# Two-layer encoder trunk on one core: direct part of the output product by pairs of row blocks, and three preparations of the second layer formed later

## The chip, the core and the metric

The kernel runs on one core of one Trainium2 chip. TensorE (PE in the profile) multiplies matrices and transposes, PEld loads its weights, VectorE (DVE) and ScalarE (ACT) work on elements, GpSimd (POOL) does small arithmetic and the DMAs that add, SyncE (SP) issues most other DMAs. The metric is the device time of one execution in microseconds (us): the median of the runs of a kernel.

## The reference

512 tokens of width 1024 go through two layers in float32. Each layer norms the tokens, projects them once into mixer heads, memory queries and gates, attends (layer one: three dilated windows; layer two: grouped queries with 2-D rotary tables), attends to 256 memory tokens, gates the heads and adds an output product to the residual stream:

```python
for i in range(DEPTH):
    h = rmsnorm(x, norm_g[i])
    mem_h = rmsnorm(mem, mem_norm_g[i])
    ...
    o_mem = memory_attention(q_mem, mem_h, w_mem_kv[i], mem_qn_g[i], mem_kn_g[i])
    y = jnp.concatenate([o_mix, o_mem], axis=-1) * jax.nn.silu(gate)
    x = x + jnp.einsum('bse,ed->bsd', y, w_out[i])
```

`y` is 512 x 1536 and `w_out[i]` is 1536 x 1024.

## The kernel before

**Numbers.** Every float32 operand of a product is split into a high part (ACT rounds it to fp32r) and a low part (DVE subtracts the high part from the original). A product is then three matmuls: high by high, low by high, high by low. For weights this is the cast `wh<-wl` (L295) and the split `wo<-wl,wh` (L305), once for each piece of 128 x 1024; a ring of four such pairs is live (`RING`).

**Strassen.** Products of 1024 columns in the inner dimension are done by quarters with seven products instead of eight (`s_chunk`): 12, 11, S1, S2, S4, S3, 22, in this order on PE. The token side needs sums of quarters (`first_t`, `diffs_t`, `rest_t`: S1 = 21 - 22, S2 = S1 - 11, S4 = S2 + 12, S3 = 11 - 21), the weight side needs T1 to T4, formed in part by DMAs that add (POOL, L260 to L279). S4 is the fifth product. Between products ACT copies a PSUM bank out (L372) and DVE adds others (L389); S2 adds into the bank that held 11, so it waits until L389 has read that.

**The output product.** The 1536 columns of `y` are taken as 1024 by Strassen and as 512 directly (`out_rest`). Strassen's results are added by DMAs into `acc`, four row blocks b of 128 tokens in two column halves n (L876). The direct part is eight groups of twelve matmuls, one for each (n, b), and DVE adds each to `acc[b][n]` (L756). Its weights are two pieces for each n, called O1 in `PLAN`; the loop runs over n and inside it over b, through `chunk`. When both halves of a block are there, `ev_o` stores the block (x1d, SP), norms it (`norm_1`: squares on ACT L475, root on POOL L477, L436, L437; `norm_2`: DVE L482), has PE transpose it (xT, L488) and builds the token side of layer two: blocks 0 and 1 give the quarters 11 and 12 (`first_t`: casts and low parts named h, copies named f), blocks 2 and 3 the differences.

**Start of layer two.** While this goes on, PE projects the memory to K and V (`mem_kv`, weights T2b: four pieces each for K and V, and for each of them two groups for either of two row blocks). K's blocks are normed (`head_sq`, `head_mul`: xn L578), transposed (qT) and split (`put_norm`, low part L634); V's are split at once (L656, L657). Then the first Strassen set of layer two follows, the memory queries. `setup_b` multiplies the rotary tables by the gains of q and k (L1279, L1282); their first reader is the rotation in the second set (L1336).

**What sets the order.** The program is written by a driver in slots: each group or product ends in `drv.tick()`, which runs the generators that are due; `yield n` puts a generator off by n slots. Each engine executes its instructions in the order so written. `Weights` plans loads, sums, casts and splits by the number g of the slot in which each piece is used last and needed first.

Of the kernel before, what the change touches and what calls it, by code (L numbers as in the profile page):

```python
# [13 lines left out]
ALU = mybir.AluOpType  # L14
# [6 lines left out]
QS = 128 ** -0.5  # L21
TCKW = {}
NBIG, NM4, NS2, SCRATCH = 7, 23, 14, 2048
RING, LEAD = 4, 2
BULK, ACTIVE, SET_AT, WARM, MEM_B, PREP_Y, ACC_AT, PREP_B, HALF, SET_B = 2, 2, 15, 1, 12, 1, 4, 1, {"a": 3, "b": 3, "o": 0}, 1
MEM_STEP = 1, 1
MEM_D = 4
PD = 2
EO = 2, 2, 1, 2, 2, 1
YB = {"m": (2, 2), "k": (1, 1, 1), 0: (1, 2, 1), 1: (1, 2, 1)}  # L30
# [95 lines left out]
def trunk_kernel(ctx: ExitStack, tc: tile.TileContext, x, mem, wall, norm_g, mem_norm_g, gcol,  # L126
                 qn_a, kn_a, qn_b, kn_b, ident_d, mask_d, tab_a, tab_b, out):
    nc = tc.nc
# [7 lines left out]
    drv = Driver()  # L136
# [31 lines left out]
    def mm_early(o, a, b, c, d, start):  # L168

        T.matmul(o, a, b, start=start, stop=False, skip_group_check=True)  # L170
        T.matmul(o, c, d, start=False, stop=False, skip_group_check=True)  # L171

    def mm_late(o, a, b, stop):
        T.matmul(o, a, b, start=False, stop=stop, skip_group_check=True)  # L174
# [15 lines left out]
    class Weights:  # L190
        def __init__(self):
            self.items, self.last, self.need, self.allocs, self.sums = [], [], [], [], []
            self.users = {}
            g = 0
            for c in SEQ:
                kind, d = PLAN[c], sum(pieces(k) for k in PLAN[:c])
                base = len(self.items)
                if kind in GROUPS:
                    units, nb = GROUPS[kind]
                    for u in range(units):  # L200
                        for x in (2 * u, 2 * u + 1):
                            self.items.append((c, "P", x))
                            self.last.append(g + (u + 1) * nb - 1)
                            self.allocs.append(((c, "P", x), d, kind))
                            self.users[c, "P", x] = 1
                            d += 1
                        self.need += [base + 2 * u + 2] * nb
                    g += units * nb
                else:
                    n = 1 if kind in ("W1", "W1b", "W1bs") else 2  # L210
                    at = {k: d + i * n for i, k in enumerate(("21", "11", "12", "22"))}
                    self.allocs += [((c, k, x), at[q] + x, kind) for k, q in LOADS for x in range(n)]
# [128 lines left out]
    def chunk(units, nb, group, evac, pre=None):  # L341

        ps = [None] * nb
        for u in range(units):
            w = []
            for h, l in (W.take(), W.take()):
                w += [(h[:, k * 512:(k + 1) * 512], l[:, k * 512:(k + 1) * 512]) for k in range(2)]
            for b in range(nb):
                if u == 0:
                    ps[b] = pj()  # L350
                if pre:
                    pre(u, b)
# [194 lines left out]
        V.tensor_tensor(s3, full["11", c], p, ALU.subtract)  # L547
        split(*slot(H, "S1", c), s1)

    def rest_t(H, c, ds):  # L550

        def put(k, f):
            hi, lo = slot(H, k, c)
            A.copy(hi, f)
            drv.late(lambda: V.tensor_tensor(lo, f, hi.bitcast(F32), ALU.subtract))

        s1, s2_, s4, s3, f22 = [full.pop((k, c)) for k in ("S1", "11", "12", "S3", "22")]
        V.tensor_tensor(s2_, s1, s2_, ALU.subtract)
        V.tensor_tensor(s4, s4, s2_, ALU.add)
        put("S2", s2_)  # L560
        yield ds[0]
        put("S4", s4)
        yield ds[1]
        put("S3", s3)
        yield ds[2]
        put("22", f22)
        yield 1
# [60 lines left out]
            yield 1  # L628
        Ms[layer] = M

    def put_norm(q, gain, hi, lo):

        drv.late(lambda: A.activation(hi, q, AF.Copy, scale=gain))
        drv.soon(lambda: V.scalar_tensor_tensor(lo, q, gain, hi.bitcast(F32), ALU.mult, ALU.subtract))  # L634
        yield 1

    def mem_kv(layer, M, pre=None):
        kt_ = [m4(F32R, "kmT").rearrange("p (h t) -> p h t", h=4) for _ in range(2)]
        vt_ = [m4(F32R, "vm").rearrange("p (b e) -> p b e", b=2) for _ in range(2)]

        def ev_k(b, p):
            r = head_sq(p)

            def rest():
                xn = head_mul(p, r)
                yield 2
                q = transpose4(xn)
                cs = slice(b * 128, (b + 1) * 128)
                yield from put_norm(q, gk_m[layer], kt_[0][:, :, cs], kt_[1][:, :, cs])

            drv.release(rest(), 2)
            yield 1

        def ev_v(b, p):

            A.activation(vt_[0][:, b], p, AF.Copy, scale=0.5)  # L656
            V.scalar_tensor_tensor(vt_[1][:, b], p, 0.5, vt_[0][:, b].bitcast(F32), ALU.mult, ALU.subtract)  # L657
            yield 1

        proj_t(M, NAT[:2], ev_k, pre)  # L660
        proj_t(M, NAT[:2], ev_v)
        return kt_, vt_
# [79 lines left out]

    def out_rest(ys, acc, done, evac):

        for n in range(2):
            def group(w, u, b, p):
                cs = slice(b * 128, (b + 1) * 128)
                while any(y is None for y in ys):
                    drv.tick()
                for k in range(4):  # L750
                    mm_early(p, ys[k][0][:, cs], w[k][0], ys[k][0][:, cs], w[k][1], k == 0)
                for k in range(4):
                    mm_late(p, ys[k][1][:, cs], w[k][0], k == 3)

            def ev(b, p, n=n):
                V.tensor_tensor(acc[b][n], p, acc[b][n], ALU.add)  # L756
                yield 1
                while (n, b) not in done:
                    yield 1
                yield from evac(n, b, acc[b])  # L760
            chunk(1, 4, group, ev)


    def gates(od, o_done):

# [485 lines left out]
    def ev_o(n, b, x1):  # L1251
        if n:
            for j in range(2):
                nc.sync.dma_start(x1d[b][:, j * 512:(j + 1) * 512], x1[j])
            r = norm_1(x1)
            yield EO[0]
            norm_2(x1, r, rows["x1"])
            yield EO[1]
            if b < 2:
                first_t(H2, x1, b)  # L1260
            else:
                yield from diffs_t(H2, x1, b - 2)
                yield EO[2]
                yield from rest_t(H2, b - 2, EO[3:])

    drv.spawn(mem_norm(1), MEM_B)
    out_proj(YW, ys, xv, ev_o, lambda: [m4(name="acc") for _ in range(2)])
# [1 line left out]


    ropeB = pool.tile([128, 2048], F32, tag="tabs", name="tabs", bufs=1).rearrange("p (a c b e) -> p a c b e", a=2, c=2, b=4)
    tb_raw = s2(name="tbraw").rearrange("p (c b e) -> p c b e", c=2, b=4)
    nc.sync.dma_start(tb_raw, tab_b.rearrange("p (c b e) -> p c b e", c=2, b=4))
    grB = s2(name="grB")[:, 0:256].rearrange("p (a e) -> p a e", a=2)
    nc.sync.dma_start(grB[:, 0], qn_b.to_broadcast([128, 128]))
    nc.sync.dma_start(grB[:, 1], kn_b.to_broadcast([128, 128]))

    def setup_b():
        V.tensor_scalar(grB[:, 0], grB[:, 0], QS, None, ALU.mult)  # L1279
        for qk in range(2):  # L1280
            for cs_ in range(2):
                V.tensor_tensor(ropeB[:, qk, cs_].rearrange("p b (h e) -> p b h e", h=2),  # L1282
                                tb_raw[:, cs_, :, None, :].to_broadcast([128, 4, 2, 64]),
                                grB[:, qk].rearrange("p (h e) -> p h e", h=2)[:, None].to_broadcast([128, 4, 2, 64]), ALU.mult)
                yield 1
# [289 lines left out]
```

## Time and profile before

| | |
|---|---|
| median of three runs | 966.98 us (965.21 to 967.11) |
| profiled execution | 968.3 us, of which the span is 966.5 us |
| granted TensorE clock, mean | 0.996 |
| PE busy | 946.8 us, 98% of the span |
| DVE, ACT, POOL busy | 82%, 71%, 35% of the span |
| direct part, layer one | about 619 to 644 us from the span's start |
| memory K and V of layer two | 644 to 672 us |
| first Strassen set of layer two | 672 to 699 us |

Times in the profile count from the start of the span. A row of the timeline gives start, duration, engine, line, operation, out<-in and shape; a bracket at its end gives the idle time of the engine before it and what ended it. Lines are those of the kernel before; in the changed kernel the same code stands 1 to 33 lines further down.

### The profile page before, as it was taken

To read this page: it belongs to the slowest core of one execution; us is meant where nothing else is said; L and a number is where in the kernel's file an instruction comes from. 1 tells how busy PE (TensorE), PEld (TensorE's weight loads), DVE (VectorE), ACT (ScalarE), POOL (GpSimd) and SP (SyncE) were. 2 spreads that over 40 slices of the span, in tenths; PEclk is the share of its full clock that TensorE was granted. 3 is DMA by queue.
4 is the path that set the end of the run, shared out by engine and by line. 5 is a ranking of instruction groups with operands and counts; after the bars stand their busy time and mean duration, and the time that the engine had idled before them with its cause. 6 is when DMAs were issued, how large, how long until landed. Compare 5 with 4: busy or idle time off the path is not lost.

```text
span 966.5 us, 16604 instructions
## 1 busy us (share of the span) xinstructions
PE 946.8 (98%) x5682; PEld 833.2 (86%) x5682; DVE 791.4 (82%) x1411; ACT 681.7 (71%) x1701; POOL 341.4 (35%) x482
## 2 busy tenths in 40 slices
PE   8999999999999999999999999999899999999998
PEld 5879888888888888888899997788899999998886
DVE  5898676878888888888888999769878898769883
ACT  5775689686868686868685657546768977879770
POOL 1512423557554545454726011322332330111010
PEclk9999999999999999999999999999899999999999
DMA  9989956969686868685959889889766687777744
GB/s 360 317 235 327 271 116 172 294 120 268 149 258 143 262 150 258 154 261 132 283 132 241 266 206 297 268 242 366 167 157 129 199 235 179 207 204 190 206 131 131
DMA packets 89129, 209.81 MB, mean 217 GB/s; under 512 B 25298, under 2 KB 36050, under 8 KB 89044
## 3 DMA queue, kind: packets, MB, share of 16 engines
q1 hardware_dynamic: 69892, 145.76, 43.4%
q0 software_dynamic: 17856, 60.83, 33.4%
q10 hardware_dynamic: 1296, 2.16, 0.6%
q8 instruction: 45, 0.74, 0.3%
q14 instruction: 40, 0.33, 0.1%
HBM read 157.27 MB, written 12.65 MB: 176 GB/s over the span
## 4 chain that ended last, share of the span: by engine, by line
PE 80%; DVE 8%; DMA 6%; ACT 3%; issue 2%; POOL 1%; SPq 0%; DVEq 0%; POOLq 0%; ACTq 0%
PE pj L170 21%; PE pj L171 21%; PE pj L174 20%; DVE wo L305 2%; PE qT L585 2%; PE sa L1106 1%; PE oo L1208 1%; PE pt L1187 1%; PE sa L1102 1%; PE ptb L1405 1%; DMA og<-odb 1%; DMA acc<-sn 1%; DMA wl<-wl 1%; DMA grB<-in_qn_b_dram 1%; DMA od<-o 1%
## 5 line engine op out<-in xcount | busy, mean ns | idle before, releaser
L305 DVE TENSOR_TENSOR wo<-wl,wh 128x1024 fp32r<-128x1024 f32 x255 | 315.1, 1242 | 6.0 <-ACT wh L295 5.8
L295 ACT CAST wh<-wl 128x1024 fp32r<-128x1024 f32 x255 | 268.5, 1060 | 29.3 <-PE pj L171 18.9
L170 PE MATMUL pj<-wh,hS 128*128 128x512 f32 (+1 forms) x448 | 159.0, 368 | 3.9 <-DVE sn L389 3.9
L171 PE MATMUL pj<-wh,hS 128*128 128x512 f32 (+1 forms) x448 | 153.6, 356 | 0.0
L170 PE MATMUL pj<-wh,h 128*128 128x512 f32 (+1 forms) x336 | 117.9, 365 | 0.0
L171 PE MATMUL pj<-wh,h 128*128 128x512 f32 (+1 forms) x336 | 114.0, 353 | 0.0
L437 POOL TENSOR_TENSOR rstd<-mse,half 128x4 f32<-128x4 f32 (+2 forms) x98 | 103.1, 1052 | 8.2
L174 PE MATMUL pj<-wo,hS 128*128 128x512 f32 (+1 forms) x448 | 100.8, 355 | 2.0 <-DVE wo L305 2.0
L170 PEld LDWEIGHTS pj<-wh,hS 128*128 128x128 f32 x448 | 85.9, 192 | 14.8 <-issue 2.6
L171 PEld LDWEIGHTS pj<-wh,hS 128*128 128x128 f32 x448 | 86.1, 192 | 10.3
L372 ACT COPY sn<-pj 128x512 f32<-128x512 f32 x132 | 73.1, 590 | 29.7 <-PE pj L174 29.7
L436 POOL TENSOR_SCALAR mse<-hss 128x4 f32<-128x4 f32 (+1 forms) x86 | 45.1, 525 | 132.2 <-ACT junk L573 128.0
L174 PEld LDWEIGHTS pj<-wo,hS 128*128 128x128 f32 x448 | 75.3, 191 | 14.5 <-DVE wo L305 2.7
L573 ACT ACTIVATE junk<-sn 128x128 f32<-128x128 f32 x264 | 79.1, 308 | 4.1 <-DVE sn L383 4.1
L1050 POOL TENSOR_TENSOR ta<-sn,tabs 128x128 f32<-128x128 f32 (+1 forms) x64 | 37.4, 592 | 118.6 <-DVE sn L578 92.0
L389 DVE TENSOR_TENSOR sn<-pj,sn 128x512 f32<-128x512 f32 x99 | 67.7, 686 | 12.3 <-PE pj L174 11.8
L174 PE MATMUL pj<-wo,h 128*128 128x512 f32 (+1 forms) x336 | 74.8, 352 | 0.0
L171 PEld LDWEIGHTS pj<-wh,h 128*128 128x128 f32 x336 | 63.8, 190 | 7.4
L170 PEld LDWEIGHTS pj<-wh,h 128*128 128x128 f32 x336 | 63.6, 189 | 7.4 <-DVE sn L389 0.2
L279 POOL DMA_DIRECT2D wl<-wl x33 | 29.1, 881 | 111.9 <-DVE wo L305 56.0
L174 PEld LDWEIGHTS pj<-wo,h 128*128 128x128 f32 x336 | 56.0, 189 | 8.7
L578 DVE TENSOR_TENSOR sn<-sn,rstd 128x512 f32<-128x512 f32 (+1 forms) x82 | 48.0, 594 | 7.2 <-POOL rstd L437 7.2
(235 smaller groups left out, 2335.1 us busy)
## 6 DMA issues: line engine op xcount, KB each, us to landing
wl<-in_wall_dram SPq DMA_DIRECT2D x222, 512.0 KB, 7.0
wl<-wl POOLq DMA_DIRECT2D x66, 512.0 KB, 5.5
wl<-in_wall_dram POOLq DMA_DIRECT2D x42, 512.0 KB, 8.5
acc<-sn POOLq DMA_DIRECT2D x16, 256.0 KB, 4.8
od<-o SPq DMA_DIRECT2D x12, 256.0 KB, 5.6
og<-od SPq DMA_DIRECT2D x12, 256.0 KB, 5.5
odb<-o SPq DMA_DIRECT2D x12, 256.0 KB, 3.4
og<-odb SPq DMA_DIRECT2D x12, 256.0 KB, 4.2
```

The lines of the kernel that those rows point to most:

```text
L170: T.matmul(o, a, b, start=start, stop=False, skip_group_check=True)
L171: T.matmul(o, c, d, start=False, stop=False, skip_group_check=True)
L174: T.matmul(o, a, b, start=False, stop=stop, skip_group_check=True)
L295: A.copy(wh, self.tile[self.items[i]])
L305: V.tensor_tensor(wo, self.tile[key], wh.bitcast(F32), ALU.subtract)
L372: A.copy(t, b)
L389: V.tensor_tensor(t, b, t, ALU.subtract if q == "12" else ALU.add)
L436: G.tensor_scalar(e, ss, EPS, None, ALU.add)
L437: G.tensor_tensor(r, e, half[:, 0:n], ALU.pow)
L573: A.activation(jk, p[:, j * 128:(j + 1) * 128], AF.Square, scale=QS, accum_out=ss[:, j:j + 1])
L578: V.tensor_tensor(xn[:, 0:n], p.rearrange("p (a b) -> p a b", a=4)[:, 0:n], r[:, 0:n, None].to_broadcast([128, n, 128]), ALU.mult)
L1050: G.tensor_tensor(ta[:, 0:n], xn[:, 0:n, 0:32], ropeA[:, 0, b, s0:s0 + n], ALU.mult)
```

## The change

1. `out_rest` runs over pairs of row blocks first, then over n, then over the two blocks. All four O1 pieces are taken in its first four groups and stay in use until the sixth and eighth group; the planner counts so.
2. `rest_t` of layer two adds S4 one slot later, in a slot of its own.
3. The low part of memory K in layer two comes five slots later, that of V's second block three.
4. The tables: their DMAs are issued inside `setup_b`, which starts at slot 9 instead of 1 after the output product, and the multiplications come four slots after that, k's before q's.

```diff
-BULK, ..., SET_B = ..., 1
+BULK, ..., SET_B = ..., 9
+LO_K, LO_V = (0, 5), (0, 3)
...
                     units, nb = GROUPS[kind]
+                    if kind == "O1":
+                        n = PLAN[c - 1] == "O1"
+                        for x in range(2):
+                            self.items.append((c, "P", x))
+                            self.last.append(g + 5)
...
+                        self.need += [base + 2] * 2 if not n else [base + 2] * 6
+                        g += 2 if not n else 6
+                        units = 0
...
-    def rest_t(H, c, ds):
+    def rest_t(H, c, ds, spread=False):
...
-        V.tensor_tensor(s4, s4, s2_, ALU.add)
+        if not spread:
+            V.tensor_tensor(s4, s4, s2_, ALU.add)
         put("S2", s2_)
-        yield ds[0]
+        if spread:
+            yield ds[0] - 1
+            V.tensor_tensor(s4, s4, s2_, ALU.add)
+            yield 1
...
-    def put_norm(q, gain, hi, lo):
+    def put_norm(q, gain, hi, lo, wait=0):
         drv.late(lambda: A.activation(hi, q, AF.Copy, scale=gain))
+        if wait:
+            yield wait
         drv.soon(lambda: V.scalar_tensor_tensor(lo, q, gain, hi.bitcast(F32), ALU.mult, ALU.subtract))
...
             A.activation(vt_[0][:, b], p, AF.Copy, scale=0.5)
+            if b and LO_V[layer]:
+                yield LO_V[layer]
...
     def out_rest(ys, acc, done, evac):
-        for n in range(2):
...
-            chunk(1, 4, group, ev)
+        ws = []
+        for bs in ((0, 1), (2, 3)):
+            for n in range(2):
+                if len(ws) == n:
+                    ws.append([])
+                    for h, l in (W.take(), W.take()):
+                        ws[n] += [(h[:, k * 512:(k + 1) * 512], l[:, k * 512:(k + 1) * 512]) for k in range(2)]
+                w = ws[n]
+                for b in bs:
...
+                    drv.release(ev(n, b, p), 2)
+                    W.advance()
+                    drv.tick()
...
-    tb_raw = s2(name="tbraw").rearrange("p (c b e) -> p c b e", c=2, b=4)
-    nc.sync.dma_start(tb_raw, tab_b.rearrange("p (c b e) -> p c b e", c=2, b=4))
...
     def setup_b():
-        V.tensor_scalar(grB[:, 0], grB[:, 0], QS, None, ALU.mult)
-        for qk in range(2):
+        tb_raw = s2(name="tbraw").rearrange("p (c b e) -> p c b e", c=2, b=4)
+        nc.sync.dma_start(tb_raw, tab_b.rearrange("p (c b e) -> p c b e", c=2, b=4))
...
+        yield 4
+        for qk in (1, 0):
+            if not qk:
+                V.tensor_scalar(grB[:, 0], grB[:, 0], QS, None, ALU.mult)
```

The order on three places, before and after. On DVE from the direct part to the norms of the blocks (acc<-pj the sums, acc<-acc,rstd the norms, wo the weight splits, tabs and grB the tables), before:

```order
L756 TENSOR_TENSOR acc<-pj,acc 128x512 x4
L305 TENSOR_TENSOR wo<-wl,wh 128x1024 x2
L482 TENSOR_SCALAR acc<-acc,rstd,row 128x512 x2
L1279 TENSOR_SCALAR grB<-grB 128x128
L1282 TENSOR_TENSOR tabs<-tbraw,grB 128x512
L482 TENSOR_SCALAR acc<-acc,rstd,row 128x512 x2
L1282 TENSOR_TENSOR tabs<-tbraw,grB 128x512
L305 TENSOR_TENSOR wo<-wl,wh 128x1024 x2
```

and after, from the same place:

```order
L767 TENSOR_TENSOR acc<-pj,acc 128x512 x4
L316 TENSOR_TENSOR wo<-wl,wh 128x1024 x2
L493 TENSOR_SCALAR acc<-acc,rstd,row 128x512 x2
L767 TENSOR_TENSOR acc<-pj,acc 128x512
L493 TENSOR_SCALAR acc<-acc,rstd,row 128x512 x2
L767 TENSOR_TENSOR acc<-pj,acc 128x512
L316 TENSOR_TENSOR wo<-wl,wh 128x1024 x2
L162 TENSOR_TENSOR h_7826<-xT,h_7826 128x4x128
```

The tables are gone from here, and the norms of blocks 0 and 1 stand among the last two sums of the direct part.

On ACT in the same place (sq the squares of a block, wh the weight casts, h and f the casts and copies of `first_t`, junk the squares of memory K), before:

```order
L475 ACTIVATE sq,ss<-acc 128x512 x4
L295 COPY wh<-wl 128x1024 x2
L475 ACTIVATE sq,ss<-acc 128x512 x2
L158 COPY h_7898<-xT 128x4x128
L158 COPY h_7906<-xT 128x4x128
L537 COPY f_7914<-xT 128x512
L537 COPY f_7916<-xT 128x512
L573 ACTIVATE junk,hss<-pj 128x128 x4
```

and after (h_7826 comes twice, for block 0 and for block 1):

```order
L306 COPY wh<-wl 128x1024 x2
L159 COPY h_7826<-xT 128x4x128
L159 COPY h_7834<-xT 128x4x128
L548 COPY f_7842<-xT 128x512
L548 COPY f_7844<-xT 128x512
L486 ACTIVATE sq,ss<-acc 128x512 x2
L306 COPY wh<-wl 128x1024 x2
L159 COPY h_7826<-xT 128x4x128
```

Block 0's casts and copies now stand ahead of the squares of blocks 2 and 3; before they stood behind them.

On DVE from V's first low part (vm) to the instruction that frees the bank for S2 (sn<-pj,sn), before:

```order
L657 TENSOR_SCALAR vm<-pj,vm 128x512
L634 TENSOR_SCALAR kmT<-qT,gc,kmT 128x4x128
L558 TENSOR_TENSOR f_7968<-fS_8078,f_7968 128x512
L559 TENSOR_TENSOR f_7966<-f_7966,f_7968 128x512
L555 TENSOR_TENSOR hS_8076<-f_7968,hS_8076 128x4x128
L657 TENSOR_SCALAR vm<-pj,vm 128x512
L305 TENSOR_TENSOR wo<-wl,wh 128x1024 x2
L634 TENSOR_SCALAR kmT<-qT,gc,kmT 128x4x128
L555 TENSOR_TENSOR hS_8161<-f_7914,hS_8161 128x4x128
L555 TENSOR_TENSOR hS_8161<-f_7966,hS_8161 128x4x128
L389 TENSOR_TENSOR sn<-pj,sn 128x512
```

and after:

```order
L678 TENSOR_SCALAR vm<-pj,vm 128x512
L575 TENSOR_TENSOR f_7842<-f_7842,f_7844 128x512
L569 TENSOR_TENSOR f_7895<-fS_8067,f_7895 128x512
L566 TENSOR_TENSOR hS_8065<-f_7895,hS_8065 128x4x128
L316 TENSOR_TENSOR wo<-wl,wh 128x1024 x2
L575 TENSOR_TENSOR f_7893<-f_7893,f_7895 128x512
L566 TENSOR_TENSOR hS_8147<-f_7842,hS_8147 128x4x128
L566 TENSOR_TENSOR hS_8147<-f_7893,hS_8147 128x4x128
L400 TENSOR_TENSOR sn<-pj,sn 128x512
```

Both low parts of K and the second of V are no longer ahead of it; the two sums for S4 (f_7842, f_7893) stand one place further back.

More of the change, by code (lines that the diff above doesn't have):

```diff
@@ L24 @@
 RING, LEAD = 4, 2
-BULK, ACTIVE, SET_AT, WARM, MEM_B, PREP_Y, ACC_AT, PREP_B, HALF, SET_B = 2, 2, 15, 1, 12, 1, 4, 1, {"a": 3, "b": 3, "o": 0}, 1
+BULK, ACTIVE, SET_AT, WARM, MEM_B, PREP_Y, ACC_AT, PREP_B, HALF, SET_B = 2, 2, 15, 1, 12, 1, 4, 1, {"a": 3, "b": 3, "o": 0}, 9
 MEM_STEP = 1, 1
 MEM_D = 4
+LO_K, LO_V = (0, 5), (0, 3)
 PD = 2
@@ L199, in __init__ @@
                     units, nb = GROUPS[kind]
+                    if kind == "O1":
[3 more added lines that the diff above has]
+                            self.last.append(g + 5)
+                            self.allocs.append(((c, "P", x), d + x, kind))
+                            self.users[c, "P", x] = 1
+                        self.need += [base + 2] * 2 if not n else [base + 2] * 6
+                        g += 2 if not n else 6
+                        units = 0
                     for u in range(units):
@@ L558, in rest_t @@
         V.tensor_tensor(s2_, s1, s2_, ALU.subtract)
-        V.tensor_tensor(s4, s4, s2_, ALU.add)
+        if not spread:
+            V.tensor_tensor(s4, s4, s2_, ALU.add)
         put("S2", s2_)
-        yield ds[0]
+        if spread:
+            yield ds[0] - 1
+            V.tensor_tensor(s4, s4, s2_, ALU.add)
+            yield 1
+        else:
+            yield ds[0]
         put("S4", s4)
@@ L648, in rest @@
                 cs = slice(b * 128, (b + 1) * 128)
-                yield from put_norm(q, gk_m[layer], kt_[0][:, :, cs], kt_[1][:, :, cs])
+                yield from put_norm(q, gk_m[layer], kt_[0][:, :, cs], kt_[1][:, :, cs], LO_K[layer])
             drv.release(rest(), 2)
@@ L743, in out_rest, with ev @@
     def out_rest(ys, acc, done, evac):
-        for n in range(2):
-            def group(w, u, b, p):
-                cs = slice(b * 128, (b + 1) * 128)
-                while any(y is None for y in ys):
-                    drv.tick()
[L750 to L760, printed above, removed]
-            chunk(1, 4, group, ev)
+        def ev(n, b, p):
+            V.tensor_tensor(acc[b][n], p, acc[b][n], ALU.add)
+            yield 1
+            while (n, b) not in done:
+                yield 1
+            yield from evac(n, b, acc[b])
+        ws = []
[7 more added lines that the diff above has]
+                for b in bs:
+                    cs = slice(b * 128, (b + 1) * 128)
+                    while any(y is None for y in ys):
+                        drv.tick()
+                    p = pj()
+                    for k in range(4):
+                        mm_early(p, ys[k][0][:, cs], w[k][0], ys[k][0][:, cs], w[k][1], k == 0)
+                    for k in range(4):
+                        mm_late(p, ys[k][1][:, cs], w[k][0], k == 3)
+                    drv.free()
+                    drv.release(ev(n, b, p), 2)
+                    W.advance()
+                    drv.tick()
     def gates(od, o_done):
@@ L1263, in ev_o @@
                 yield EO[2]
-                yield from rest_t(H2, b - 2, EO[3:])
+                yield from rest_t(H2, b - 2, EO[3:], True)
     drv.spawn(mem_norm(1), MEM_B)
@@ L1271, in trunk_kernel @@
     ropeB = pool.tile([128, 2048], F32, tag="tabs", name="tabs", bufs=1).rearrange("p (a c b e) -> p a c b e", a=2, c=2, b=4)
-    tb_raw = s2(name="tbraw").rearrange("p (c b e) -> p c b e", c=2, b=4)
-    nc.sync.dma_start(tb_raw, tab_b.rearrange("p (c b e) -> p c b e", c=2, b=4))
-    grB = s2(name="grB")[:, 0:256].rearrange("p (a e) -> p a e", a=2)
-    nc.sync.dma_start(grB[:, 0], qn_b.to_broadcast([128, 128]))
-    nc.sync.dma_start(grB[:, 1], kn_b.to_broadcast([128, 128]))
-    def setup_b():
-        V.tensor_scalar(grB[:, 0], grB[:, 0], QS, None, ALU.mult)
-        for qk in range(2):
+    def setup_b():
+        tb_raw = s2(name="tbraw").rearrange("p (c b e) -> p c b e", c=2, b=4)
+        nc.sync.dma_start(tb_raw, tab_b.rearrange("p (c b e) -> p c b e", c=2, b=4))
+        grB = s2(name="grB")[:, 0:256].rearrange("p (a e) -> p a e", a=2)
+        nc.sync.dma_start(grB[:, 0], qn_b.to_broadcast([128, 128]))
+        nc.sync.dma_start(grB[:, 1], kn_b.to_broadcast([128, 128]))
+        yield 4
+        for qk in (1, 0):
+            if not qk:
+                V.tensor_scalar(grB[:, 0], grB[:, 0], QS, None, ALU.mult)
             for cs_ in range(2):
```

## Prediction

> **What bounds the kernel now.** I read the page first, then the PE's rows for its gaps, a table by 5 us windows around the gaps, the chain of waits, and the rows of DVE, ACT and POOL there. From the page:
>
> ```profile
> span 966.5 us, 16604 instructions
> PE 946.8 (98%) x5682; PEld 833.2 (86%) x5682; DVE 791.4 (82%) x1411; ACT 681.7 (71%) x1701; POOL 341.4 (35%) x482
> ```
>
> TensorE is busy 98% of the span, so a change that removes no matmul can gain only in its gaps. The largest lie between the layers. Two windows there (length, then PE, PEld, DVE, ACT, POOL busy; granted clock, DMA share, GB/s):
>
> ```profile
> 680.00:685.00 5.00, 1.22 (x8) 1.02 (x8) 5.00 (x7) 5.00 (x9) 0.00 (x0) 0.83 0.73 171
> 685.00:690.00 5.00, 4.75 (x22) 4.78 (x23) 5.00 (x7) 2.20 (x10) 2.71 (x1) 0.50 0.24 66
> ```
>
> From 680 to 685 PE worked 1.22 us of 5 while DVE was full, and the clock fell to half. PE's rows (start, duration, instruction; in brackets the idle time before it and what ended it); the starts at 677.66, 685.25, 690.34 and 696.10 are those of the products S1, S2, S4 and 22 of the first Strassen set of layer two:
>
> ```profile
> 593.67 0.50 PE L170 MATMUL pj<-wh,yS 128*128 128x512 f32 x1 [1.68 <-DVE sn L389]
> 664.57 1.06 PE L488 MATMUL xT<-ident,acc 128*128 128x128 f32 x8 [1.32 <-DVE acc L482]
> 677.66 0.28 PE L170 MATMUL pj<-wh,hS 128*128 128x256 f32 x1
> 681.56 1.22 PE L174 MATMUL pj<-wo,hS 128*128 128x256 f32 x8 [1.81 <-DVE wo L305]
> 685.25 0.55 PE L170 MATMUL pj<-wh,hS 128*128 128x256 f32 x1 [2.47 <-DVE sn L389]
> 690.34 0.28 PE L170 MATMUL pj<-wh,hS 128*128 128x256 f32 x1
> 696.10 0.28 PE L170 MATMUL pj<-wh,h 128*128 128x256 f32 x1
> ```
>
> Three waits (1.32, 1.81, 2.47 us), all ended by DVE. S4 and S3 took 5.76 us together, so an undisturbed product takes 2.88; S2, at half clock, took 690.34 - 685.25 = 5.09, which is 2.21 more. Without any of it, 22 would start at 677.66 - 1.32 + 4 x 2.88 = 687.86 instead of 696.10: 8.2 us is the ceiling of what can be had here.
>
> Why is DVE late? The chain of waits passes through one DMA there (start, length, link):
>
> ```profile
> 642.72 8.06 DMA grB<-in_qn_b_dram
> ```
>
> and DVE's own rows say what stood in its queue:
>
> ```profile
> 650.80 0.23 DVE L1279 TENSOR_SCALAR grB<-grB 128x128 f32<-128x128 f32 x1 [2.15 <-DMA grB<-in_qn_b_dram]
> 662.42 0.68 DVE L1282 TENSOR_TENSOR tabs<-tbraw,grB 128x512 f32<-128x512 f32 x1
> 663.02 1.41 DVE L482 SCALAR_TENSOR_TENSOR acc<-acc,rstd,row 128x512 f32<-128x512 f32 x2
> 664.34 0.69 DVE L578 TENSOR_TENSOR xn<-pj,rstd 128x512 f32<-128x512 f32 x1
> 676.57 0.74 DVE L634 SCALAR_TENSOR_TENSOR kmT<-qT,gc,kmT 128x512 fp32r<-128x512 f32 x1
> 679.68 0.69 DVE L657 SCALAR_TENSOR_TENSOR vm<-pj,vm 128x512 fp32r<-128x512 f32 x1 [0.38 <-ACT vm L656]
> 682.55 0.75 DVE L634 SCALAR_TENSOR_TENSOR kmT<-qT,gc,kmT 128x512 fp32r<-128x512 f32 x1
> 684.42 0.69 DVE L389 TENSOR_TENSOR sn<-pj,sn 128x512 f32<-128x512 f32 x1
> 685.02 1.22 DVE L305 TENSOR_TENSOR wo<-wl,wh 128x1024 fp32r<-128x1024 f32 x1
> ```
>
> DVE stood 2.15 us for the gains of the tables, wrote four table pieces that nobody needs yet (one shown), and came late to the norm of the fourth row block (L482 at 663.02, PE's 1.32 us) and to K's first block (xn at 664.34). From there 20.68 us of queue (664.34 to 685.02) led to L389, which frees the bank that S2 adds into.
>
> **The change, part by part.**
>
> *Low parts of memory K and V.* The order moves three of these four DVE instructions behind L389: both L634 and the second L657. Neighbours overlap by 0.09 us (L389 runs 0.69, the next starts 0.60 after it), so they held the queue 0.65, 0.66 and 0.60 us, and the second L657 brought 0.38 of waiting: 2.29 us. From xn to the instruction after L389 remain 20.68 - 2.29 = 18.39 us. The fifth product's sum (L559) only trades places within that stretch: nothing either way.
>
> *Tables and pairs of blocks.* These decide when xn starts. Rows for that walk (the wait on grB is gone, so it goes by what each step waits for instead):
>
> ```profile
> 638.65 0.39 PE L170 MATMUL pj<-wh,y 128*128 128x512 f32 x1
> 644.09 0.39 PE L170 MATMUL pj<-wh,act 128*128 128x512 f32 x1
> 659.48 1.03 PE L488 MATMUL xT<-ident,acc 128*128 128x128 f32 x8
> 658.68 2.02 ACT L295 CAST wh<-wl 128x1024 fp32r<-128x1024 f32 x2
> 652.89 1.07 ACT L158 CAST h<-xT 128x512 fp32r<-128x512 f32 x2 [1.42 <-PE xT L488]
> 656.59 1.19 ACT L537 COPY f<-xT 128x512 f32<-128x512 f32 x2 [2.63 <-DVE h L161]
> 646.41 0.62 ACT L475 ACTIVATE sq<-acc 128x512 f32<-128x512 f32 x1
> 652.58 0.93 POOL L437 TENSOR_TENSOR rstd<-mse,half 128x1 f32<-128x1 f32 x1
> 651.54 0.26 POOL L477 TENSOR_TENSOR mse<-ss 128x1 f32<-128x1 f32 x1 [1.34 <-ACT sq L475]
> 653.61 0.94 POOL L269 DMA_DIRECT2D wl<-wl  x1
> 659.26 1.05 POOL L437 TENSOR_TENSOR rstd<-mse,half 128x4 f32<-128x4 f32 x1
> ```
>
> The pairs order holds the first two pieces of the direct part for six groups, so K's first two casts cannot start before group six ends at 638.65; DVE splits them until about 642.1 (2.35 a pair). Two norms (1.41 each) and two sums into acc (0.6 each) bring it to 646.1. K's other pieces come free when the direct part ends, 644.09; cast by 646.1, split by 648.5. Block 0's transposes run after group one of K, and its two low parts (0.6 each) follow by 649.7. Block 1's wait for ACT, which first has block 0's copies (1.19, to 650.4, since each follows its low part), block 2's squares (two of 0.62) and two casts (2.02) to do: its own casts (1.07) end at 654.7, the low parts at 655.5. V's first pieces: 657.8. The norm of block 2 ends at 659.2, just ahead of its transposes, which PE can start at 659.48 as before (two blocks were transposed by then in either order). Block 3's squares follow block 1's copies on ACT and end at 657.4, its rstd on POOL 2.0 us later (651.54 to 653.51 in the rows), its norm at 660.9, well ahead of its transposes, due at 664.57 - 1.32 = 663.25: the 1.32 us go. POOL then issues T2's summing DMA (0.94) and makes K's rstd (1.4 with its first step): xn at 661.8, 2.5 us earlier than 664.34. Its bounds: 660.3, when K's rstd was there before (659.26 + 1.05), and 664.34, if ACT's order eats all of it.
>
> So S2 can start at 661.8 + 18.39 + 0.23 (685.02 to 685.25 in the rows) = 680.4. PE could start it at 677.66 - 1.32 + 2.88 = 679.2, so 1.2 us of wait stay, and 22 starts at 680.4 + 3 x 2.88 = 689.0 instead of 696.10: 7.1 us gained.
>
> Does so short a wait leave the clock alone? At 593.67 PE had stood 1.68 us and the 2.47 us wait is the one in which the clock fell, 3.7 us after another of 1.81; I take no drop for 1.2. [...]
>
> *What is moved behind.* The table writes now follow the products:
>
> ```profile
> 692.63 0.69 DVE L555 TENSOR_TENSOR h<-f,h 128x512 fp32r<-128x512 f32 x1 [2.31 <-ACT h L554]
> 714.27 0.69 DVE L1336 TENSOR_TENSOR ta<-sn,tabs 128x512 f32<-128x512 f32 x1
> ```
>
> Five table instructions and the three low parts are 4.6 us. DVE had 2.31 us idle in one piece there, and the first reader of the tables came at 714.27, 20 us on: in that time seven products' worth of PE work covers the rest, so they stay hidden. Uncovered they would cost between 0 and 4.6; below 0 is excluded, since nothing is removed there. I take 0. The tables' DMAs now stand on SP behind five weight loads, but are due some 30 us later than their issue in the walk; block 0 and 1's stores stand ahead of four loads the first of which is cast only at 658.68, which costs nothing.
>
> *Direct part itself.* The second product's pieces are needed two groups earlier. In layer one and at the end of the program:
>
> ```profile
> 626.77 1.21 DVE L305 TENSOR_TENSOR wo<-wl,wh 128x1024 fp32r<-128x1024 f32 x1
> 626.78 0.48 PE L170 MATMUL pj<-wh,y 128*128 128x512 f32 x1
> 945.47 1.22 DVE L305 TENSOR_TENSOR wo<-wl,wh 128x1024 fp32r<-128x1024 f32 x1
> 946.08 0.39 PE L170 MATMUL pj<-wh,y 128*128 128x512 f32 x1
> ```
>
> Group three starts at 626.78 and reads the last low part in its sixth matmul, 1.2 us on, just as the split ends (627.98): 0.1 us at most. At the end 946.08 + 1.14 = 947.2 against 946.69: nothing. The last group and what follows it stay as they are.
>
> Sum: 7.1 - 0.1 = 7.0 us. The profiled execution took 968.3 us (span 966.5 and 1.8 around it), 1.3 above the median of 966.98; it would take 961.3, and the median 960.0.
>
> **The rivals.**
> - *No wait is left.* ACT and POOL deliver sooner than walked (xn at 660.3 would do): 22 at 687.86, gain 8.1, 958.9 us.
> - *The half clock stays.* Either a wait of 1.2 us and another short one close by are enough (1.81 and 2.47 were), or the fall has another cause than the waits: S2 takes 5.09, 22 starts at 680.4 + 5.09 + 5.76 = 691.25, gain 4.8: 962.2 us. Against it: 1.68 us at 593.67 did nothing. [...]
> - *xn comes no earlier.* DVE now waits for ACT at block 1 instead of for the tables, and xn stays at 664.34: S2 at 664.34 + 18.62 = 683.0, 3.8 us of wait, half clock, 22 at 693.8; gain 2.2: 964.8 us. For it: ACT too was full, 5.00 of 5 us, from 680 to 685. Against it: the walk has DVE idle for 4.5 us at block 1 and xn still 2.5 us sooner.
> - *Slower: T2's summing DMA lands too late.* POOL issues it after block 3's rstd, at 653.61 before and about 659.5 now. T2's cast stands in ACT's queue ahead of S2's second half, and from its landing it takes 7.1 us to S2 (cast 1.0, S2's cast 0.6 and low part 0.6, two splits 2.3, four short ones 2.4, 0.2). From a landing at 673.3 on S2 moves with it, and beyond 678.1, 18.6 us after issue, the kernel is slower; at 22 us S2 starts at 688.6 and the time is 970.3. Issues near it:
>
> ```profile
> wl<-wl POOLq DMA_DIRECT2D x1, 512.0 KB, 8.7
> wl<-in_wall_dram POOLq DMA_DIRECT2D x1, 512.0 KB, 11.5
> ```
>
> 8.7 us was this DMA itself; 11.5 was a sum issued at 672.33, the slowest of the stretch. Against 18.6 the margin is 7 us.
>
> **How the numbers follow.** Forecast 0.60; no wait left 0.10; half clock stays 0.10; xn no earlier 0.12; T2 late 0.08. 0.2%, about what a measurement of this kernel tells from no change, is 1.9 us. The first three are faster; xn no earlier lies at its edge and is split 0.05 to faster and 0.07 to the same: faster 0.85, same 0.07, slower 0.08. The range reaches from 957.6 (no wait left and a us from later short waits that may close) to 965.0 (xn no earlier).
>
> **What would show it.** Right: no wait on grB on DVE, no idle before block 3's transposes, xn near 662, L389 three places sooner, one wait before S2 of 1 to 1.5 us, clock 1.00 throughout there, 22 near 689, and the rest shifted as a block. Wrong: a granted clock of 0.5 near 680, POOL or ACT rows waiting on a weight DMA between 665 and 685, a new PE gap after 690 that a table write ended, or one in the last direct part.

## The result and the profile after

| | before | after |
|---|---|---|
| median | 967.24 us (965.21 to 973.76, 22 runs) | 964.40 us (962.17 to 967.89, 22 runs) |
| profiled execution | 968.3 us, span 966.5, clock 0.996 | 965.53 us, span 963.8, clock 1.000 |

The ratio is 0.9964, 95% interval 0.9953 to 0.9975: faster by 2.8 us where 7.0 were forecast. The median lies inside the forecast range (957.6 to 965.0), near the end that stood for "xn comes no earlier"; that is luck, since neither that rival's wait of 3.8 us nor its half clock is in the trace. From the page of the changed kernel:

```profile
span 963.8 us, 16606 instructions
PE 945.9 (98%) x5682; PEld 832.0 (86%) x5682; DVE 791.0 (82%) x1411; ACT 682.1 (71%) x1701; POOL 341.5 (35%) x482
```

The two windows in which TensorE stood idle and then ran at half clock (length, busy time of PE, PEld, DVE, ACT, POOL; granted clock, DMA share, GB/s):

```profile
680.00:685.00 5.00, 3.35 (x28) 3.17 (x28) 4.92 (x7) 4.39 (x8) 0.00 (x0) 1.00 0.92 300
685.00:690.00 5.00, 5.00 (x44) 5.00 (x44) 5.00 (x8) 4.26 (x13) 3.41 (x4) 1.00 0.47 134
```

Busy time went from 1.22 to 3.35 us in the first, and the clock is whole in both. PE's rows of the changed kernel: the first product of layer two's K (the row at 644.09 before), S2, 22, and one in layer two's output product:

```profile
646.01 0.39 PE L171 MATMUL pj<-wh,act 128*128 128x512 f32 x1
682.72 0.35 PE L171 MATMUL pj<-wh,hS 128*128 128x256 f32 x1 [1.66 <-ACT hS L565]
691.43 0.28 PE L171 MATMUL pj<-wh,h 128*128 128x256 f32 x1
909.78 0.50 PE L171 MATMUL pj<-wh,yS 128*128 128x512 f32 x1 [2.35 <-DVE sn L400]
```

And DVE's rows: the wait at block 1, the norm of block 3, K's xn, one new wait, the instruction that frees S2's bank (L389 before, L400 now), and in layer two's output product the wait for the heads' rows (og):

```profile
655.53 1.29 DVE L162 TENSOR_TENSOR h<-xT,h 128x512 fp32r<-128x512 f32 x2 [4.26 <-ACT h L159]
660.88 1.42 DVE L493 SCALAR_TENSOR_TENSOR acc<-acc,rstd,row 128x512 f32<-128x512 f32 x2 [0.46 <-POOL rstd L448]
663.54 0.69 DVE L595 TENSOR_TENSOR xn<-pj,rstd 128x512 f32<-128x512 f32 x1 [1.25 <-POOL rstd L448]
677.03 0.69 DVE L566 TENSOR_TENSOR hS<-f,hS 128x512 fp32r<-128x512 f32 x1 [0.69 <-ACT hS L565]
681.89 0.68 DVE L400 TENSOR_TENSOR sn<-pj,sn 128x512 f32<-128x512 f32 x1
907.17 0.69 DVE L829 TENSOR_TENSOR sn<-sn,og 128x512 f32<-128x512 f32 x1 [4.83 <-DMA og<-odb]
```

Between the layers nearly everything stands where the prediction put it: no wait on grB, no idle before block 3's transposes, one wait ahead of S2, full clock. Counted from K's first product, 22 comes 691.43 - 646.01 = 45.42 us later, where the forecast had 689.0 - 644.09 = 44.91 and the shown execution of before had 52.01. That stretch is shorter by 6.59 us. The span is shorter by only 2.77, since K started 1.92 later (646.01 against 644.09) and from 22 to the end it took 272.33 instead of 270.43, 1.90 more: 6.59 - 1.92 - 1.90 = 2.77. Of the later start, 1.26 us were there before the direct part began: the same matmuls of layer one's output product start at 601.05 before and at 602.31 after. The experiments ask what the two losses are.

### The profile page after: what moved, and what is told of

It is laid out like the page before. It is cut to its first block, busy times and chain, and to the rows that moved or that the text cites. A ratio compares the mean times of both kernels' runs of the same rounds, so it can differ in the third digit from the quotient of the medians.

```text
span 963.8 us, 16606 instructions
## 1 busy us (share of the span) xinstructions
PE 945.9 (98%) x5682; PEld 832.0 (86%) x5682; DVE 791.0 (82%) x1411; ACT 682.1 (71%) x1701; POOL 341.5 (35%) x482
## 4 chain that ended last, share of the span: by engine, by line
PE 88%; DVE 6%; DMA 4%; ACT 2%; issue 1%; SPq 0%; DVEq 0%; ACTq 0%
PE pj L171 23%; PE pj L175 23%; PE pj L172 23%; PE qT L602 2%; PE sa L1137 1%; PE oo L1239 1%; DMA od<-o 1%; PE pt L1218 1%; DVE wo L316 1%; PE sa L1133 1%; PE ptb L1438 1%; DMA og<-odb 1%; PE xT L499 1%; PE row L623 1%; PE ob L175 1%
## 5 line engine op out<-in xcount | busy, mean ns | idle before, releaser
L171 PEld LDWEIGHTS pj<-wh,hS 128*128 128x128 f32 x448 | 84.8, 189 | 14.1 <-DVE sn L400 1.9
L172 PEld LDWEIGHTS pj<-wh,hS 128*128 128x128 f32 x448 | 84.9, 190 | 10.2
L400 DVE TENSOR_TENSOR sn<-pj,sn 128x512 f32<-128x512 f32 x99 | 67.7, 685 | 11.3 <-PE pj L175 10.9
```

The lines of the kernel that those rows point to most:

```text
L400: V.tensor_tensor(t, b, t, ALU.subtract if q == "12" else ALU.add)
```

## The experiments

The table holds, for each kernel's profiled execution, K's first product (start), from it to K's first xn, from xn to the instruction that frees S2's bank, from K to S2, from S2 to 22, from K to 22 and from 22 to the span's end, all in us, as differences of starts, and then the median time. They were taken from starts in nanoseconds, so the last digit can differ by 0.01 from the rows shown. The medians come from four measurements, in which the kernel before itself had 966.82 to 968.17 us; the ratios given below are to before in the same measurement.

| kernel | K at | K-xn | xn-bank | K-S2 | S2-22 | K-22 | 22-end | median |
|---|---|---|---|---|---|---|---|---|
| before, as shown | 644.09 | 20.25 | 20.07 | 41.16 | 10.85 | 52.01 | 270.4 | 967.24 |
| before, again | 646.97 | 18.02 | 20.07 | 38.92 | 10.86 | 49.78 | 270.2 | 968.27 |
| before, tables' DMAs early | 645.62 | 18.02 | 20.07 | 38.92 | 11.03 | 49.96 | 269.8 | 967.05 |
| before, accumulators later | 646.31 | 18.11 | 20.07 | 39.01 | 10.19 | 49.20 | 269.1 | 966.21 |
| before + pairs | 648.30 | 19.34 | 20.08 | 40.26 | 10.92 | 51.18 | 270.1 | 968.70 |
| after, tables early | 646.35 | 19.35 | 18.35 | 38.53 | 11.21 | 49.74 | 270.2 | 967.43 |
| after, low parts early | 646.37 | 17.54 | 20.73 | 39.10 | 10.19 | 49.30 | 269.5 | 967.68 |
| after | 646.01 | 17.54 | 18.34 | 36.71 | 8.71 | 45.42 | 272.3 | 964.40 |
| after, again | 645.81 | 17.53 | 18.34 | 36.71 | 8.71 | 45.41 | 271.2 | 963.78 |
| after, sum in its old slot | 645.06 | 17.54 | 18.05 | 36.42 | 8.71 | 45.13 | 270.5 | 963.13 |
| after, no pairs | 645.32 | 17.30 | 18.34 | 36.46 | 8.71 | 45.17 | 270.6 | 963.54 |
| after, accumulators later | 645.09 | 17.55 | 18.35 | 36.72 | 8.70 | 45.43 | 269.1 | 961.74 |
| after, no pairs, accum. later | 644.35 | 17.29 | 18.34 | 36.47 | 8.70 | 45.17 | 269.1 | 961.17 |
| the same, S4 one slot later still | 646.18 | 17.30 | 18.04 | 36.18 | 9.47 | 45.65 | 270.5 | 963.57 |

The first loss shows no sign of being a cost of the change: K starts between 644.09 and 648.30 in the five traces of the kernel before and its variants, and between 644.35 and 646.37 in the nine of the changed one. 644.09, the execution that the prediction read, is the earliest of all.

**Both kernels again.** No edit.

> The kernel before, unchanged, for more executions and a second trace. Theory A (what went is systematic): the three waits between the layers (1.3, 1.8, 2.5 us) and the half clock of S2 stand in this trace too, most executions show a granted clock near 0.996, and 22 starts some 18.4 us after S1. Theory B (the half clock was a chance of the one execution shown): the waits stand, but S2 takes about 2.9 us in place of 5.1, 22 starts about 16.2 us after S1, and most executions show 0.999 to 1.000; then 2.2 of the forecast 7.0 us never were there in a typical execution. Both: 967.2 us, within 0.5.

> The changed kernel, unchanged, for a second trace. Theory C (what was given back in layer two's output product, a wait of 2.35 us ended by L400 where the trace of before has 0.74, belongs to that execution): the wait there is 0.7 to 0.9 us now; between the layers one wait of 1.4 to 1.9 us, 18.35 us from xn to L400's start, full clock. Theory H (the earlier PE runs into the DMAs of that place): 2 us or more of wait there again. Time 964.4 within 0.7 by both.

Before measured 968.27 us (ratio to itself 1.0003, 0.9989 to 1.0017), after 963.78 (0.9957, 0.9940 to 0.9974). PE's rows of the second trace of before (K, the wait in S1, S2, 22), then DVE's (the table's gains, xn):

```profile
646.97 0.39 PE L170 MATMUL pj<-wh,act 128*128 128x512 f32 x1
682.21 1.21 PE L174 MATMUL pj<-wo,hS 128*128 128x256 f32 x8 [1.13 <-DVE wo L305]
685.90 0.55 PE L170 MATMUL pj<-wh,hS 128*128 128x256 f32 x1 [2.48 <-DVE sn L389]
696.75 0.28 PE L170 MATMUL pj<-wh,h 128*128 128x256 f32 x1
651.45 0.22 DVE L1279 TENSOR_SCALAR grB<-grB 128x128 f32<-128x128 f32 x1
664.99 0.69 DVE L578 TENSOR_TENSOR xn<-pj,rstd 128x512 f32<-128x512 f32 x1
```

The clock still fell here, so Theory B falls. But Theory A holds only in part: of the three waits that the prediction listed, the one ahead of block 3's transposes (1.32 us) is not there at all, the second is 1.13 instead of 1.81, and only the one ahead of S2 is the same. grB has no wait either, and K to xn took 18.02 us instead of 20.25. In the execution first shown K had started 2.9 us earlier, and DVE spent 2.15 us of that waiting for the DMA; 22 came only 0.65 us sooner (696.10 against 696.75). The DMA of grB landed at 650.8 us there, and at 651.0 and 650.9 in the two other traces of the kernel before in which it is issued at the same place (before again, before with the accumulators later), though K started 2.9 and 2.2 us later in these: it did not come sooner for PE being early. Of the changed kernel two traces agree to 0.01 us in every step up to 22, so what varies is when PE arrives, and what the program makes of it.

**The wait itself taken away.** In the kernel before, only the place of three DMAs on SP changes; DVE's order stays.

```diff
+    ropeB = ...; tb_raw = ...; nc.sync.dma_start(tb_raw, ...)
+    grB = ...; nc.sync.dma_start(grB[:, 0], ...); nc.sync.dma_start(grB[:, 1], ...)
     drv.spawn(mem_norm(1), MEM_B)
     out_proj(YW, ys, xv, ev_o, ...)
-    ropeB = ...; tb_raw = ...; (the same lines)
```

> The kernel before, with the tables' three DMAs issued ahead of the output product of layer one; DVE's order stays, so that only the wait on grB goes. Prediction's reading (the 2.15 us that DVE stood for grB made it late for block 3 and xn): xn up to 2.1 us earlier by PE's own entry, 965 to 966 us. Theory D (that wait appeared only because PE came 2 to 3 us earlier to this place in that execution than in the others; with PE later DVE has no wait there): no change, 967.2 to 968.2 us, and from PE's start of layer two's K to xn the same as in the second trace of the kernel before.

967.05 us, ratio 0.9996 (0.9982 to 1.0010): nothing gained that can be told from noise. Its DVE rows:

```profile
650.10 0.22 DVE L1279 TENSOR_SCALAR grB<-grB 128x128 f32<-128x128 f32 x1
663.64 0.68 DVE L578 TENSOR_TENSOR xn<-pj,rstd 128x512 f32<-128x512 f32 x1
```

From K (645.62) to xn it is 18.02 us, the figure of the second trace of before. Theory D holds: the 2.15 us were the slack of one early execution, not a cost of the kernel.

**Tables early, low parts early.** Two parts of the change undone, one at a time.

```diff
-..., SET_B = ..., 9        # and setup_b with its own DMAs, k before q
+..., SET_B = ..., 1        # and setup_b as before
```

```diff
-LO_K, LO_V = (0, 5), (0, 3)
+LO_K, LO_V = (0, 0), (0, 0)
```

> The changed kernel with the rotary tables' DMAs and DVE writes early, as before. Reading of the trace after: DVE has 4.3 us idle at block 1, which takes the first piece and the wait for its DMA; two pieces stand ahead of block 3's norm, and xn waits 1.2 us for POOL anyway: it costs at most 0.5 us, 964.4 to 964.9. Rival (the prediction's reading: the wait on grB and the four pieces are what made DVE late): 2.1 us of wait and two pieces of 0.65 come back ahead of xn, up to 3 us: 966.5 to 967.5.

> The changed kernel with the low parts of the memory's K and of V's second block formed at once, as before. Theory A: three DVE instructions and a wait, 2.3 us, stand ahead of L400 again, the one wait ahead of S2 grows from 1.7 to about 3.9 us: 966.7 us at full clock. [...] Rival 2 (ACT's hS, which ended S2's wait, and not DVE decides): the wait stays within 0.5 us of 1.7, 964.4.

967.43 us (ratio 0.9994, 0.9971 to 1.0017) and 967.68 (0.9989, 0.9976 to 1.0001): either part undone takes nearly the whole gain. PE's waits in the two, tables first:

```profile
681.07 1.22 PE L175 MATMUL pj<-wo,hS 128*128 128x256 f32 x8 [0.32 <-DVE wo L316]
684.88 0.55 PE L171 MATMUL pj<-wh,hS 128*128 128x256 f32 x1 [2.59 <-ACT hS L565]
681.01 1.22 PE L175 MATMUL pj<-wo,hS 128*128 128x256 f32 x8 [0.54 <-DVE wo L316]
685.48 0.36 PE L171 MATMUL pj<-wh,hS 128*128 128x256 f32 x1 [3.25 <-ACT hS L565]
```

DVE's rows with the tables early (table pieces and K's xn):

```profile
657.08 0.68 DVE L1313 TENSOR_TENSOR tabs<-tbraw,grB 128x512 f32<-128x512 f32 x1
661.28 1.28 DVE L1313 TENSOR_TENSOR tabs<-tbraw,grB 128x512 f32<-128x512 f32 x2
665.70 0.69 DVE L595 TENSOR_TENSOR xn<-pj,rstd 128x512 f32<-128x512 f32 x1 [1.26 <-POOL rstd L448]
```

The table pieces put xn 1.81 us later (19.35 against 17.54), not through a wait on grB (there is none in that trace): one ahead of block 2's norm and two ahead of block 3's are about 1.9 us, and the waits for POOL behind them move along. The first expectation (at most 0.5) was wrong; the rival had the size but not the cause. The low parts put S2's bank 2.39 us later (20.73 against 18.34), as Theory A had it, but the clock fell as well, which Theory A had left at full. Both versions run S2 at half clock (0.50 in the windows from 684 to 690 with the tables early, from 686 to 688 with the low parts early): S2 to 22 took 11.21 and 10.19 us instead of 8.71. So, in the changed kernel, each part is worth some 2 us by itself, and the 1.5 to 2.5 us from S2 to 22 need both. How long the clock was low, in windows of 2 us: before first, then the low parts early.

```profile
682.00:684.00 2.00, 0.78 (x7) 0.57 (x5) 2.00 (x4) 2.00 (x5) 0.00 (x0) 0.82 0.43 70
684.00:686.00 2.00, 0.75 (x3) 0.78 (x4) 2.00 (x3) 2.00 (x5) 0.00 (x0) 0.50 0.53 215
686.00:688.00 2.00, 2.00 (x12) 2.00 (x11) 2.00 (x4) 1.20 (x9) 0.70 (x1) 0.50 0.00 0
688.00:690.00 2.00, 2.00 (x11) 2.00 (x11) 2.00 (x3) 0.00 (x0) 2.00 (x1) 0.50 0.39 82
690.00:692.00 2.00, 2.00 (x18) 2.00 (x17) 0.31 (x1) 1.46 (x3) 1.92 (x3) 0.97 0.47 188
684.00:686.00 2.00, 0.53 (x4) 0.56 (x5) 1.96 (x3) 2.00 (x5) 0.00 (x0) 0.96 1.03 422
686.00:688.00 2.00, 2.00 (x11) 2.00 (x11) 2.00 (x3) 2.00 (x4) 0.00 (x0) 0.50 0.81 326
688.00:690.00 2.00, 2.00 (x14) 2.00 (x13) 2.00 (x4) 1.12 (x8) 0.70 (x2) 0.68 0.34 78
```

In the trace before, windows of 0.2 us from 682 to 691 all show 1.00 or 0.50, save the two in which the clock changes (0.70 at 683.20, 0.73 at 690.00). So a window of 2 us at 0.82 held (1 - 0.82) / 0.5 x 2 = 0.72 us of half clock; summed that way it lasted 6.84 us before and 3.44 us with the low parts early.

**The pairs, alone and left out; the sum in its old slot.** The first and second edit put out_rest of before into the changed kernel and the new out_rest into the kernel before, each with its planning of the weight ring; the third:

```diff
-                yield from rest_t(H2, b - 2, EO[3:], True)
+                yield from rest_t(H2, b - 2, EO[3:])
```

> The changed kernel with the direct part by column halves as before (one edit of four undone). Theory A (the pairs bring K's first xn forward): xn comes 2.5 us later, the wait ahead of S2 grows from 1.7 to about 4.2 us: 966.9 us, or 969.1 if the clock halves in it. Rival (xn is set by POOL's rstd and ACT's queue, not by the direct part): the wait ahead of S2 stays within 0.5 us of 1.7 and the time stays at 964.4.

> The kernel before with the pairs of row blocks alone. Prediction's reading (the pairs bring block 2, block 3 and K's xn forward): S2 sooner by up to 2 us, 965.2 to 966 us. Theory E, from the version without the late tables (by PE's entry its xn was 1.3 us later than in the second trace of the kernel before): two table pieces now stand ahead of block 3's norm and xn waits for POOL behind it; S2 1.3 us later, half clock as before: 968.5 us.

> The changed kernel with the fifth product's sum formed in its old slot. The prediction put nothing on it: 964.1 us within 0.4, the wait ahead of S2 1.7. Rival: the sums stand ahead of S2's own low parts again, S2's second half is cast 0.6 us later and S2 with it: 964.7.

Without the pairs 963.54 us (ratio 0.9958, 0.9938 to 0.9979), the pairs alone 968.70 (1.0009, 0.9993 to 1.0026), the sum in its old slot 963.13 (0.9959, 0.9943 to 0.9974). For the first the rival holds (1.41 us of wait ahead of S2). The pairs bring nothing: by the table they cost 0.24 us in K to xn in the changed kernel (17.54 against 17.30). In the kernel before xn comes 1.32 us later with them (19.34 against 18.02), as Theory E had it; the time, 1.0009, could not tell that from no change. DVE's rows of that kernel:

```profile
663.22 1.29 DVE L1302 TENSOR_TENSOR tabs<-tbraw,grB 128x512 f32<-128x512 f32 x2
664.97 1.42 DVE L492 SCALAR_TENSOR_TENSOR acc<-acc,rstd,row 128x512 f32<-128x512 f32 x2 [0.46 <-POOL rstd L447]
667.64 0.69 DVE L588 TENSOR_TENSOR xn<-pj,rstd 128x512 f32<-128x512 f32 x1 [1.26 <-POOL rstd L447]
```

Two table pieces ahead of block 3's norm, and the waits on POOL come after them all the same. Pairs and tables thus belong together: late tables bring K's xn 1.81 us forward with the pairs (19.35 to 17.54) and 0.72 without them (18.02 to 17.30), so more than half of the 1.81 us is there only in the order of the pairs. The moved sum costs 0.29 us in xn to bank (18.34 against 18.05), too little to show in the time. Both expectations missed here: without the move the wait ahead of S2 was 1.36 us, shorter and not the same or longer.

**The accumulators' loads in layer two's output product.** The trace after had a wait of 2.35 us at 909.78, its second trace one of 1.23, less than Theory H and more than Theory C expected; before had 0.74. SP's queue there in the changed kernel (start, time at SP, issue; the last two rows are the kernel before):

```profile
894.29 0.33 SPq L1328 DMA_DIRECT2D odb<-o  x1
898.45 0.38 SPq L811 DMA_DIRECT2D og<-odb  x1
898.88 2.05 SPq L899 DMA_DIRECT2D acc<-x1d  x2
900.98 0.43 SPq L811 DMA_DIRECT2D og<-odb  x1
902.20 0.93 SPq L868 DMA_DIRECT2D acc<-x1d  x2
903.17 0.43 SPq L780 DMA_DIRECT2D og<-odb  x1
```

Two of the four loads of the accumulators (512 KB each) are issued between the two halves of og, for which DVE waits. The order is the same in the kernel before, but there the two loads held SP 0.93 us and not 2.05. The edit lets them come one slot later:

```diff
-        drv.spawn(load(), ACC_AT)
+        drv.spawn(load(), ACC_AT if src is xv else 5)
```

> The changed kernel, with the loads of the accumulators in layer two's output product one slot later, so that SP issues the second half of the heads' rows ahead of them; nothing else moves. Theory H (SP's order and the DMAs there cost the 2.35 us each time): the wait ended by L400 near 908 us falls below 0.8 and the time to about 962.5. Theory C (2.35 was that execution's): at most 0.7 us gained, 963.7 to 964.4.

> The kernel before, with the accumulators' loads of layer two's output product one slot later (the same edit as in the version of the changed kernel that gained). If the wait there is one that the change made worse: before loses only its own wait of 0.3 to 0.8 us, 966.6 us. If the place costs the same in both kernels: 2.0 to 2.6 us gained, 964.8 us.

> The changed kernel without the pairs and with the accumulators' loads later. If the pairs are worth nothing once tables and low parts are late: 961.7 us, as with the pairs. If the pairs cost something (963.54 without them against 964.4 and 963.78 with them): 961.0.

```profile
892.84 0.33 SPq L1328 DMA_DIRECT2D odb<-o  x1
895.37 0.89 SPq L811 DMA_DIRECT2D og<-odb  x2
896.31 0.93 SPq L899 DMA_DIRECT2D acc<-x1d  x2
```

These rows are of the changed kernel with the edit: 961.74 us, ratio 0.9948 (0.9930 to 0.9966), and PE's wait there is gone, as Theory H had it. The changed kernel without the edit had 963.78 in the same measurement. In the traces, 22 to the end is 269.1 us, 2.1 to 3.3 less than in the two without the edit. The kernel before, with the same edit, measured 966.21 against 966.82 (0.9987, 0.9971 to 1.0004), its stretch 0.8 to 1.4 us shorter than in its other traces: nearer to the first expectation (966.6) than to the second (964.8). So what was given back there can be had again. That the change itself makes the wait longer is not shown: without the pairs it was 0.78 us, with the sum in its old slot 0.97, hardly more than before (0.74), and 22 to the end was 270.6 and 270.5 as before. Why the DMAs took longer in the trace after (the store odb landed 4.0 us after its issue, 3.0 before) was not separated. With the pairs left out too the time is 961.17 us, ratio 0.9932 (0.9915 to 0.9950), the lowest of all, though the interval overlaps that with the pairs; it does not decide between 961.7 and 961.0.

**One more step on S4.** The changed kernel without pairs, with the accumulators later, and:

```diff
-                yield from rest_t(H2, b - 2, EO[3:], True)
+                yield from rest_t(H2, b - 2, (3, 2, 1), True)
```

> The changed kernel without the pairs, with the accumulators' loads later as above, and with the fourth Strassen product's sums and second low part one slot later again (3, 2, 1 in place of 2, 2, 1), which puts L400's counterpart one low part (0.6 us) sooner in DVE's queue. Theory A: the wait ahead of S2 falls from 1.4 to about 0.8 us, the one near 907 from 0.8 to 0, together 1 us below the version without pairs: 962.5 us. Rival (S2 is held by ACT's cast, or the product after it is late in turn): no change to that version, 963.5.

963.57 us (0.9965, 0.9952 to 0.9978): 2.4 us more than the same kernel without this step (961.17). The wait ahead of S2 fell to 1.12 us, but PE now waited 0.51 for S3's low part (689.93) and 1.06 for 22's (694.13), together 1.57. The rival holds: the products behind are late in turn. The rest of the 2.4 us was not traced.

## Why the prediction was wrong

- **Low parts: right.** Forecast 2.29 us off the stretch from xn; undone alone they cost 2.39 (20.73 against 18.34). The whole stretch shrank less, from 20.07 to 18.34, by 1.73, as DVE got a new wait of 0.69 us on ACT's cast of hS (677.03). Of that the moved sum of the fifth product, which the forecast put at "nothing either way", brought a part: in its old slot the wait is 0.25 and the stretch 18.05.
- **The wait ahead of S2 and the clock: right.** 1.2 us forecast, 1.66 measured, clock 1.00; S2 to 22 went from 10.86 to 8.71, 2.15 against 2.21 forecast. It does not hold in every execution, on either side. Half clock for 3.4 us lowers the mean clock of an execution by 3.4 x 0.5 / 966 = 0.0018, to 0.998, and for 6.8 us to 0.996 (measured: 0.998 with the 3.44 us of the low parts early, 0.996 with the 6.84 of the trace before). In 4 of the 22 runs of the changed kernel the mean clock was 0.998, and those took 966.1 to 967.9 us. Of the 35 runs of before that were measured beside its second trace none reached 0.999, but 11 had 0.998; in the trace of before with the accumulators later, which has 3.4 us of half clock, S2 to 22 took 10.19 us, only 1.48 more than 8.71.
- **Failed: "xn at 661.8, 2.5 us earlier than 664.34".** The walk to xn was right (17.71 us from K, measured 17.54); what it was compared with was not. 664.34 held 2.2 us of waiting on grB that came from one early arrival of PE, and the 1.32 us ahead of block 3's transposes stand in that trace alone; in its other traces, late or early DMAs alike, K to xn is 18.0 to 18.1, so late tables and pairs together gave 0.5 us there. "DVE stood 2.15 us for the gains" was read as the cause, and with the wait taken away nothing changed. The tables do matter, by their pieces on DVE, and the pairs bring nothing.
- **Failed, smaller: "the rest shifted as a block".** 22 to the end took 0.8 to 1.9 us longer in the two traces than in the first one of before (270.4), most of it in PE's wait behind og (1.23 and 2.35 us against 0.74). What makes that wait longer stays open.
- With both put right: 0.5 + 1.7 + 2.15 = 4.4 us typically gained up to 22, less 0.8 to 1.9, is 2.5 to 3.6; the medians say 2.8 and 3.5.
- The slower rival (T2's DMA) did not appear: no wait of PE above 0.25 us between 22 and 873 us in the trace after.

## What to carry to other kernels

Before a wait in a profile is counted as a gain, ask whether the waiting engine, or the one that feeds it, had only come early: a second execution of the same kernel shows it, as does an edit that removes the wait alone. Count stretches from a point on the engine that binds (here K's first product), since absolute times carry the chance of all that went before (K started between 644.09 and 648.30 us in the traces of before and its variants). And when a stretch gets shorter, look at the next place where that engine meets DMAs that have their own pace (that of grB landed at 650.8 to 651.0 us, with K's start anywhere from 644.09 to 646.97); the issue order on the queue there may now decide (here 22 to the end was 271.2 and 272.3 us, and 269.1 with the accumulators' loads later).

## What the runs showed of the hardware

The half clock lasted one of two times. Summed over windows of 2 us, it lasted 6.80 to 6.84 us in five traces (before twice, before with the tables' DMAs early, before with the pairs, after with the tables early) and 3.40 to 3.44 in two (after with the low parts early, before with the accumulators later). The longer time is twice the shorter within 0.08 us. In the trace before it was one unbroken stretch, from about 683.3 to 690.1. What sets the two times was not shown.

In these traces the length of a single wait did not by itself decide whether the clock fell. In the trace before, the low clock began 0.72 us ahead of 684.00, at about 683.3, when PE had stood only 0.5 us of the 2.47 ahead of S2 (from 685.25 - 2.47 = 682.78). With the low parts early it began at about 685.8, 0.4 us after the wait of 3.25 had ended. It did not fall in the traces with 1.65 to 1.67 us ahead of S2, nor at the 2.35 us at 909.78 (1.00 in the windows of 2 us from 905 to 915). In the five traces of the kernel before and its variants the clock fell with no wait above 2.47 or 2.48 us, each time with a shorter one (1.13 to 2.17 us) some 3.7 us ahead. What makes the clock fall was not separated.
